# Queries projected in one pass over four banks, and two more steps by sums fed by moved weight preparations

## The chip, the cores and the metric

The kernel runs on one core of a Trainium2 chip. Its time is the device time of one execution in microseconds (us); the median of three runs counts. The engines are named as in the profile: PE (TensorE, matrix products), ACT (ScalarE), DVE (VectorE), POOL (GpSimd), SP (SyncE, which only issues loads here).

## What is computed

One layer of a streaming encoder on 256 tokens of width 2048, in float32: a gated linear attention in chunks of 64 tokens with 4 heads, then a squared-ReLU MLP, each behind an RMSNorm, and a final RMSNorm.

```python
def _gla_mixer(h, w_in, w_gate_up, b_gate, o_norm, w_out):
    proj = h @ w_in                       # 2048 x 6160: q 1024, k 1024, v 2048, r 2048, g_low 16
    q, k, v, r, g_low = jnp.split(proj, ...)
    log_a = jax.nn.log_sigmoid(g_low @ w_gate_up + b_gate) / GATE_TEMP
    ...                                   # k decayed within its chunk, a state per head, o = q @ state
    o = o * lax.rsqrt(jnp.mean(o * o, axis=-1, keepdims=True) + EPS) * o_norm
    return (o * jax.nn.silu(r)) @ w_out   # 2048 x 2048

def _sq_relu_mlp(h, w_up, w_down):        # 2048 x 8192, 8192 x 2048
    a = jax.nn.relu(h @ w_up)
    return (a * a) @ w_down

h = x + _gla_mixer(_rmsnorm(x, gla_norm), ...)
h = h + _sq_relu_mlp(_rmsnorm(h, mlp_norm), ...)
return _rmsnorm(h, final_norm)
```

## The kernel before

Every float32 operand of a projection is split in two parts, `hi` (rounded to the type that PE takes at full rate) and `lo` (the rest), and a product is made of three: hi by hi, hi by lo, lo by hi. All weights are streamed once. For 128 or 256 rows of weights, a *step*, SP loads 512 KB into one of 6 buffers `raw`; ACT copies it into a buffer `hi` (`L123`); DVE subtracts to get `lo` (`L136` in most stages, `L170` where 512 columns of two row blocks are taken at once, `L365` for sums); PE uses the two. There are 5 buffers each of `hi` and `lo`, so ACT and DVE work a few steps ahead of PE. A matmul moves 256 columns and is one instruction; a normal step has 24 of them.

**Steps by sums.** In `group` (four value and gate groups `x_group`, four output groups `out_group`, and in another form the MLP's second half) some steps of 256 x 512 weights are multiplied as 2 x 2 blocks by Winograd's scheme: seven block products in place of eight. POOL issues an accumulating DMA that adds one weight block onto another (`L335`), DVE makes further sums in `raw` (`L233`, `L234` in `weight_sums`), and a second pair of buffers takes the split sums (`L365`). PE first does three block products (9 matmuls); the other four (12 matmuls) are `pending` and come one step later. On the other side the activations need sums too, made once for a pair of row blocks `kp`: `X_FORMED = (0, 1, 4)` for the input, `FORMED = (0, 1, 6, 7)` for the attention's output.

**Preparations.** For some steps of the output groups the weight sums are made early, in stages where DVE has time, and written to DRAM: `make_sums` gives two jobs, `high` (load, three sums on DVE: `L252`, `L233`, `L234`; copy to `hi`, `L255`; POOL writes it to DRAM, `L256`) and `low` (DVE's `L259`, then POOL's write `L260`). `MADE_OUT` lists them as (group, kp), `MADE_AT` the places of a stage where they are done. The buffers `raw`, `hi` and `lo` of a preparation come from the same pools as those of the weight steps, so a `hi` of it is free for the next use when its write to DRAM has landed.

**Stages**, with their time in the profile: the first half of the values with the gate's low rank (4.5 to 51 us), keys (51.6 to 95.6), queries (95.6 to 139.8; two halves of 512 columns, each in two PSUM banks), the values' second half as groups V0 and V1 (139.8 to 167.7 to 188.4; the attention's scores are done within V0), the output gate's first half as groups G0 and G1 with the attention in them (to 238), its second half R (to 283), four output groups (to 371), the MLP (to 1009 and the tail).

The order within a stage is written by hand: `side` holds small jobs (gate, decays, sums of squares) of which `pump` takes one after each row block, `jobs` holds the preparations, `V0`, `V1`, `G0`, `G1` and `ORDER` give the order of the `kp` in a group and which go by sums, `between` what is done behind a step. The order on each engine then follows the program's, shifted by a scheduler; a buffer of a pool is given to the next tile that the scheduler sees fit. `OFF` and `even` place an operand at an address whose remainder by 128 bytes is 64 or, on purpose, 0; `FIRST` lets a group's first products take such a tile (`xe`).

Of the kernel before, what the change touches and what calls it, by code (L numbers as in the profile page):

```python
# [32 lines left out]
P = 128  # L33
T = 256
# [3 lines left out]
KT = D // P  # L38
# [3 lines left out]
KEYW = HEADS * DK  # L42
# [5 lines left out]
G = 1024  # L48
GT = 512
# [11 lines left out]
OFF = 48  # L61
# [8 lines left out]
def tile_gla_mlp(ctx, tc, x, xt, cols, w_vg, w_in, w_gate, w_out, w_up, w_down, final_norm, out):  # L70
    nc = tc.nc
# [53 lines left out]
    def slots():  # L125
        return [wpool.tile([P, SLOT], F32R, tag=i, name=i) for i in ("hi", "lo")]
# [84 lines left out]
    def turned(row, w, c0, even=(0,), acc=None):  # L211

        acc = acc or acc_banks(GT // P // 2)
        for kp in range(KT // 2):
            wh, wl = pair_of(w, kp, c0, even)
            for i in range(2):
                kt = 2 * kp + i
                ah, al = row(kt)
                for j in range(GT // P):
                    s = slice(j * P, (j + 1) * P)  # L220
                    o = acc[j // 2][:, j % 2 * T : (j % 2 + 1) * T]
                    for n, (u, m) in enumerate(((wh, ah), (wh, al), (wl, ah))):

                        nc.tensor.matmul(  # L224
                            o, u[:, i, s], m, start=kt == 0 and n == 0 and j % 2 == 0,
                            stop=kt == KT - 1 and n == 2, skip_group_check=True,
                        )
                if kt < KT - 1:
                    pump()
        return acc  # L230
# [3 lines left out]
        return nc.vector.tensor_tensor(u[:, 1::2], u[:, 1::2], u[:, 2:3].to_broadcast([P, 2, T]), op=ALU.subtract)  # L234


    MADE_OUT = ((1, 1), (2, 1), (3, 1), (3, 6))
    MADE_DOWN = ()
    MADE_AT = ((2,), (4,), (6, 10))
    made = {}  # L240

    def make_sums(key, src):
# [140 lines left out]
    def rows(w, c0, n=G, r0=0):  # L383
        return lambda kt: w[r0 + kt * P : r0 + (kt + 1) * P, c0 : c0 + n]
# [56 lines left out]
    def from_bank(dst, bank):  # L441

        b = bank.rearrange("p (i t) -> p i t", i=2)
        nc.scalar.copy(dst[:, :, WRAP:T], b[:, :, : T - WRAP])
        nc.vector.tensor_copy(dst[:, :, :WRAP], b[:, :, T - WRAP :])
# [222 lines left out]
    def extend_q(c):  # L668
        nc.scalar.copy(qt[:, c, T : T + CHUNK], qt[:, c, CHUNK:P])
        nc.vector.tensor_tensor(  # L670
            qt[:, c, T + CHUNK :].rearrange("p (b s) -> p b s", b=2),
            qt[:, c, P:T].rearrange("p (b s) -> p b s", b=2),
            dq[:, c, :].unsqueeze(2).to_broadcast([P, 2, CHUNK]),
            op=ALU.mult,
        )

    make = make_all()
    for half in range(2):
        jobs.extend(next(make))
        acc = turned(stream_x, w_in, half * GT, even=())  # L680
        for b in range(2):
            c0 = 4 * half + 2 * b
            from_bank(qt[:, c0 : c0 + 2], acc[b])
        side.extend([lambda c=c: extend_q(c) for c in range(4 * half, 4 * half + 4)])


    at = big.tile([P, 2, HEADS, 3 * P + 64], F32R, tag="C", name="at")
# [43 lines left out]
    def x_group(n, c0, order, summed, between, put, rows_of={}):  # L731
# [29 lines left out]
            order, summed, between, row, at_of, combine, put_all, filled=False, rows_of=rows_of,  # L761
        )

    V0 = (5, 6, 2, 0, 7, 3, 4, 1), (0, 4)
    V1 = (2, 5, 0, 3, 4, 6, 1, 7), (0, 4, 1)
    G0 = (2, 5, 0, 3, 4, 6, 1, 7), (0, 4, 1)
    G1 = (2, 0, 5, 4, 3, 1, 6, 7), (0, 4, 1)
    FIRST = {2: ((0, 1), (0, 0), (1, 0), (1, 1)), 3: ((0, 0), (0, 1), (1, 0), (1, 1))}
    rest = [side.popleft() for _ in range(len(side))]
    at_of_v = lambda c: lambda bank, t: put_v(bank, 512, t, G + c)  # L770
    x_group(0, 3 * KEYW, *V0, {
        0: lambda: [f() for f in rest[0:2]], 2: lambda: [f() for f in rest[2:4]],
        1: lambda: two_scores(0), 4: lambda: two_scores(2),
    }, at_of_v(0), FIRST)
# [119 lines left out]
    def begin_out(g):  # L894

        for t in range(NT):
            out_banks[g, t] = bank = psum_bank(out_ids[2 * (g % 2) + t])
            nc.scalar.copy(bank, h[:, t, g * GT : (g + 1) * GT])
# [5 lines left out]
        turn(on, turned_o, gain_o, 0, forms_o),  # L904
        turn(on, turned_o, gain_o, 1, forms_o, [psum_bank(i, "aux") for i in r_banks[4:]]),
    )])
    side.extend([nothing] * 3 + [lambda i=i: load_h(i % 2, i // 2) for i in range(4)] + [lambda: begin_out(0)])
    r_banks = list(acc_free)
    out_ids = r_banks[4:] + r_banks[:4]
    acc = natural(once_x, rows(w_in, 5 * KEYW), G, HALF, order=even_at(3, 5))  # L910
# [562 lines left out]
```

## Time and profile before

| | |
|---|---|
| median of 3 runs | 1040.99 us (1039.88 to 1041.95) |
| the profiled execution's own time | 1040.84 us, of which the span of the program's instructions is 1039.1 us |
| busy | PE 99%, DVE 87%, ACT 73%, POOL 13% |
| granted PE clock | 0.998 |
| moved by DMA | 240 MB, mean 231 GB/s |

The span runs from the first to the last instruction; 1.7 us of the execution lie around it. Busy shares are of the span. In the timeline a row is a run of equal instructions: its start, how long it lasts, engine, line, what it writes and reads, how many, and in brackets the idle time ahead of it and what ended that. Matmuls overlap, so the distance of two starts is what a matmul costs, not its length.

### The profile page before, as it was taken

Reading aid. Unit: us, or ns where it says so; the run is one execution under the profiler, and the core shown is the slowest. Engines: PE = TensorE matmul, PEld = TensorE weight load, DVE = VectorE, ACT = ScalarE, POOL = GpSimd, SP = SyncE. Lnnn points to the kernel's source line nnn. Section 1 sums busy time; section 2 is a strip of 40 time slices with the busy share of each in tenths; the row PEclk is TensorE's granted clock in tenths of the full one; section 3 lists DMA queues with packets and bytes.
Section 4 is the critical chain, followed back from the end, with each engine's and each line's share of the span. In section 5 each row is a group of like instructions: output and inputs, shape, how many; then the busy total and the mean of one; then the engine's idle time right before and its main releaser. Section 6 shows DMA issues by size and latency. Waiting matters only on the chain.

```text
span 1039.1 us, 23376 instructions
## 1 busy us (share of the span) xinstructions
PE 1030.4 (99%) x9019; PEld 1029.5 (99%) x9019; DVE 903.5 (87%) x1254; ACT 754.1 (73%) x1130; POOL 134.4 (13%) x180
## 2 busy tenths in 40 slices
PE   9999999999999999999999999999999999999997
PEld 9999999999999999999999999999999999999997
DVE  7769768898698866989989999999999999999887
ACT  7775556677576654688779788778778778778685
POOL 0000110210100001111111111111211111111100
PEclk9999999999999999999999999999999999999999
DMA  9967866758977876678888887887887888887772
GB/s 340 334 192 217 263 187 170 210 163 300 308 245 251 250 249 193 189 216 229 228 239 227 231 238 225 236 242 221 245 232 221 244 225 229 243 231 219 231 246 84
DMA packets 128591, 240.04 MB, mean 231 GB/s; under 512 B 11440, under 2 KB 30000, under 8 KB 128352
## 3 DMA queue, kind: packets, MB, share of 16 engines
q1 hardware_dynamic: 107456, 215.32, 64.2%
q0 software_dynamic: 20304, 21.64, 12.2%
q10 hardware_dynamic: 720, 1.60, 0.4%
q8 instruction: 70, 1.15, 0.4%
q14 instruction: 41, 0.34, 0.1%
HBM read 232.22 MB, written 6.29 MB: 230 GB/s over the span
## 4 chain that ended last, share of the span: by engine, by line
PE 99%; issue 0%; ACT 0%; DVE 0%; POOLq 0%; POOL 0%; DVEq 0%
PE up L1021 34%; PE acc L1021 28%; PE acc L305 16%; PE acc L181 10%; PE acc L224 6%; PE aux L224 2%; PE aux L181 1%; PE aux L843 1%; PE aux L696 1%; PE aux L399 0%; ACT sqf L1360 0%; PE acc L595 0%; DVE hf L1432 0%; POOLq L1469 0%; POOL rf L521 0%
## 5 line engine op out<-in xcount | busy, mean ns | idle before, releaser
L123 ACT CAST hi<-raw 128x1024 fp32r<-128x1024 f32 (+4 forms) x654 | 518.2, 822 | 201.1 <-DVE raw L233 66.4
L136 DVE TENSOR_TENSOR lo<-raw,hi 128x768 fp32r<-128x768 f32 (+4 forms) x228 | 233.1, 1032 | 53.6 <-ACT hi L123 50.8
L1021 PE MATMUL acc<-hi,act 128*128 128x256 f32 x1696 | 247.7, 276 | 0.0
L1021 PE MATMUL up<-hh,hi 128*128 128x256 f32 x1024 | 238.7, 276 | 0.0
L1021 PE MATMUL up<-hl,hi 128*128 128x256 f32 x1024 | 238.7, 276 | 0.0
L1021 PEld LDWEIGHTS acc<-hi,act 128*128 128x128 f32 x1696 | 217.6, 188 | 0.0
L170 DVE TENSOR_TENSOR lo<-raw,hi 128x1024 fp32r<-128x1024 f32 x160 | 194.4, 1218 | 22.5 <-ACT hi L123 21.6
L1021 PEld LDWEIGHTS up<-hh,hi 128*128 128x128 f32 x1024 | 192.3, 188 | 0.0
L1021 PEld LDWEIGHTS up<-hl,hi 128*128 128x128 f32 x1024 | 192.3, 188 | 0.0
L1231 POOL DMA_DIRECT2D raw<-in_w_down x112 | 97.1, 867 | 518.4 <-DMA raw<-in_w_down 206.2
L1291 DVE TENSOR_TENSOR lo<-raw,hi 128x1024 fp32r<-128x1024 f32 x112 | 136.3, 1217 | 1.1 <-ACT hi L123 1.1
L1021 PE MATMUL up<-hh,lo 128*128 128x256 f32 x1024 | 137.0, 276 | 0.0
L1021 PE MATMUL acc<-lo,act 128*128 128x256 f32 x848 | 133.9, 276 | 0.0
L1021 PEld LDWEIGHTS up<-hh,lo 128*128 128x128 f32 x1024 | 125.7, 188 | 0.0
L1021 PEld LDWEIGHTS acc<-lo,act 128*128 128x128 f32 x848 | 113.4, 188 | 0.0
L234 DVE TENSOR_TENSOR raw<-raw 128x512 f32<-128x512 f32 x137 | 94.5, 689 | 3.4
L233 DVE TENSOR_TENSOR raw<-raw 128x256 f32<-128x256 f32 x137 | 57.8, 422 | 13.1 <-DMA raw<-in_w_out 10.1
L181 PE MATMUL acc<-hi,xA 128*128 128x256 f32 (+1 forms) x376 | 55.6, 280 | 0.0
L181 PEld LDWEIGHTS acc<-hi,xA 128*128 128x128 f32 x376 | 49.3, 188 | 0.3 <-ACT hi L123 0.2
L224 PE MATMUL acc<-xA,hi 128*128 128x256 f32 x288 | 49.2, 276 | 0.0
L224 PEld LDWEIGHTS acc<-xA,hi 128*128 128x128 f32 x288 | 43.3, 188 | 0.0
L1148 ACT COPY sums<-acc 128x512 f32<-128x512 f32 x46 | 26.8, 583 | 22.6 <-PE acc L1021 22.5
(226 smaller groups left out, 1442.2 us busy)
## 6 DMA issues: line engine op xcount, KB each, us to landing
raw<-in_w_up SPq DMA_DIRECT2D x128, 512.0 KB, 4.3
raw<-in_w_down SPq DMA_DIRECT2D x224, 256.0 KB, 4.3
raw<-in_w_in SPq DMA_DIRECT2D x69, 512.0 KB, 4.6
raw<-in_w_down POOLq DMA_DIRECT2D x112, 128.0 KB, 5.1
raw<-in_w_out SPq DMA_DIRECT2D x22, 512.0 KB, 7.1
raw<-in_w_down SPq DMA_DIRECT2D x16, 512.0 KB, 5.2
raw<-in_w_vg SPq DMA_DIRECT2D x14, 520.0 KB, 8.6
raw<-in_w_out SPq DMA_DIRECT2D x24, 256.0 KB, 5.9
```

Source lines behind the costliest of these rows:

```text
L123: last_hi[0] = nc.scalar.copy(to, raw)
L136: last_lo[0] = nc.vector.tensor_tensor(lo[:, s], raw[:, s], hi[:, s].bitcast(F32), op=ALU.subtract)
L170: last_lo[0] = nc.vector.tensor_tensor(to[1], dst, to[0].bitcast(F32), op=ALU.subtract)
L181: newest[0] = nc.tensor.matmul(o[:, m], x, w[:, m], start=first and c == 0, stop=last, skip_group_check=True).ins
L224: nc.tensor.matmul(o, u[:, i, s], m, start=kt == 0 and n == 0 and j % 2 == 0, stop=kt == KT - 1 and n == 2, skip_group_check=True,)
L233: nc.vector.tensor_tensor(u[:, 2], u[:, 0], u[:, 2], op=ALU.subtract)
L234: return nc.vector.tensor_tensor(u[:, 1::2], u[:, 1::2], u[:, 2:3].to_broadcast([P, 2, T]), op=ALU.subtract)
L305: newest[0] = nc.tensor.matmul(bank[:, o + d : o + d + T], x, w[:, d : d + T], start=(not filled or bank in sums_banks) and bank.name not ...
L1021: newest[0] = nc.tensor.matmul(o, x, w, start=first, stop=last, skip_group_check=True).ins
L1148: last_end[0] = nc.scalar.copy(to, src).ins
L1231: nc.gpsimd.dma_start(out=raw[:, :T], in_=src[:, 0, T:], accum_op=ALU.add)
L1291: last_lo[0] = nc.vector.tensor_tensor(to[1][:, :G], u, to[0][:, :G].bitcast(F32), op=ALU.subtract)
```

## The change

1. **Queries in one pass.** The two halves become one loop over 16 row blocks with 1024 columns and four PSUM banks. A step is still 512 KB and 24 matmuls, 384 in all, and DVE's and ACT's work for a step is the same. The weights' `lo` is made by `L136` rather than `L170`, `pump` takes two side jobs per step, and all four banks are copied out at the end, where before two were copied out half way. The eight `extend_q` (a copy on ACT, a product on DVE) all come after the stage, in V0.
2. **Three preparations in the query stage** where there were two, one in V0 (places 5 and 6 of its steps) where there was none, one in R where there were two: five in place of four. The new one is (2, 6).
3. **A third step by sums in V0** (`kp` 1, with another order), and **a fourth in output group 2** (`kp` 6), which takes the new preparation.
4. In R the loads of `h` are queued two row blocks earlier.

```diff
-    MADE_OUT = ((1, 1), (2, 1), (3, 1), (3, 6))
+    MADE_OUT = ((1, 1), (2, 1), (2, 6), (3, 1), (3, 6))
-    MADE_AT = ((2,), (4,), (6, 10))
+    MADE_AT = ((1, 6, 11), (5,), (10,))
...
     make = make_all()
-    for half in range(2):
-        jobs.extend(next(make))
-        acc = turned(stream_x, w_in, half * GT, even=())
-        for b in range(2):
-            c0 = 4 * half + 2 * b
-            from_bank(qt[:, c0 : c0 + 2], acc[b])
-        side.extend([lambda c=c: extend_q(c) for c in range(4 * half, 4 * half + 4)])
+    jobs.extend(next(make))
+    acc = acc_banks(4)
+    for kt in range(KT):
+        wh, wl = weights(rows(w_in, 0)(kt), G, room=[a[:, OFF : OFF + G] for a in slots()])
+        xh, xl = stream_x(kt)
+        for j in range(8):
+            o = acc[j // 2][:, j % 2 * T : (j % 2 + 1) * T]
+            for n, (u, m) in enumerate(((wh, xh), (wh, xl), (wl, xh))):
+                nc.tensor.matmul(o, u[:, j * P : (j + 1) * P], m, ...)
+        if kt < KT - 1:
+            pump(2)
+    for b in range(4):
+        from_bank(qt[:, 2 * b : 2 * b + 2], acc[b])
+    side.extend([lambda c=c: extend_q(c) for c in range(8)])
...
-    V0 = (5, 6, 2, 0, 7, 3, 4, 1), (0, 4)
+    V0 = (5, 6, 2, 0, 4, 3, 1, 7), (0, 4, 1)
...
+    now = next(make)
     rest = [side.popleft() for _ in range(len(side))]
-    x_group(0, 3 * KEYW, *V0, {
-        0: lambda: [f() for f in rest[0:2]], 2: lambda: [f() for f in rest[2:4]],
+    between = {
+        0: lambda: [f() for f in rest[0:4]], 2: lambda: [f() for f in rest[4:8]],
         1: lambda: two_scores(0), 4: lambda: two_scores(2),
-    }, at_of_v(0), FIRST)
+    }
+    x_group(0, 3 * KEYW, *V0, {i: lambda i=i: (between.get(i, nothing)(), now[i]()) for i in range(8)}, at_of_v(0), FIRST)
...
-    side.extend([nothing] * 3 + [lambda i=i: load_h(i % 2, i // 2) for i in range(4)] + [lambda: begin_out(0)])
+    side.extend([nothing] + [lambda i=i: load_h(i % 2, i // 2) for i in range(4)] + [nothing] * 2 + [lambda: begin_out(0)])
...
-        out_group(g, ORDER[1], FORMED if g == 3 else (0, 1, 7), {
+        out_group(g, ORDER[1], FORMED if g > 1 else (0, 1, 7), {
```

What the change does to POOL's queue in V0 and V1 is seen in its order; `L335` are the accumulating loads of the steps by sums, and the brackets name the semaphores that an instruction waits for (DMASW are those of POOL's own DMAs, DMAHW those of SP's). Before, the three first rows are V0's `kp` 0 and 4 and V1's `kp` 0:

```order
L335 DMA raw_1976<-in_w_in 128x256 [waits DMAHW5_49,DMAHW3_49,DMAHW7_49,DMAHW1_49,DVE_49]
L335 DMA raw_2114<-in_w_in 128x256 [waits DMAHW3_49,DMAHW4_49,DMAHW2_49,DMAHW6_49,DMAHW0_49,DVE_49]
L335 DMA raw_2254<-in_w_in 128x256 [waits DMAHW0_49,DMASW4_49,DVE_49]
L335 DMA raw_2322<-in_w_in 128x256 [waits DMAHW5_49,DMAHW3_49,DVE_49]
L335 DMA raw_2388<-in_w_in 128x256 [waits DMAHW2_49,DMAHW6_49,DMASW0_49,DVE_49]
```

With the change the three first accumulating loads are V0's `kp` 0, 4 and 1, the fourth V1's `kp` 0; the write of V0's preparation (`made_1281`) stands behind that one:

```order
L335 DMA raw_1988<-in_w_in 128x256 [waits DMAHW3_49,DMAHW4_49,DMAHW2_49,DMAHW6_49,DMAHW0_49,DVE_49]
L335 DMA raw_2009<-in_w_in 128x256 [waits DMAHW3_49,DMAHW5_49,DMAHW2_49,DMAHW7_49,DMAHW1_49,DVE_49]
L335 DMA raw_2141<-in_w_in 128x256 [waits DMAHW1_49,DMAHW6_49,DMASW0_49,DVE_49]
L335 DMA raw_2283<-in_w_in 128x256 [waits DMASW7_49,DMAHW3_49,DMASW1_49,DVE_49]
L256 DMA made_1281<-hi_2137 128x1024 [waits DMASW2_49,Activation_49]
L260 DMA made_1281<-lo_2138 128x1024 [waits DMASW3_49,DVE_49]
L335 DMA raw_2351<-in_w_in 128x256 [waits DMAHW6_49,DMAHW0_49,DMAHW7_49,DMASW4_49,DVE_49]
```

So the two writes take the places 5 and 6 of these seven, and their issue waits until the load for V1's `kp` 0 is there.

On ACT, the end of V0 before has no preparation; `hi_2163` are the sums of `kp` 4, `hi_2196` is V1's first step, `L710` the scores' copies out of PSUM (two of the eight rows are shown):

```order
L123 CAST hi_2118<-raw_2114 128x768 [waits DMAHW4_49,DMAHW3_49,PE_49]
L123 CAST hi_2135<-raw_2133 128x1024 [waits DMAHW5_49,PE_49]
L123 CAST hi_2163<-raw_2114 128x2x256 [waits DMASW5_49,DVE_49,PE_49]
L123 CAST hi_2163<-raw_2114 128x2x256 [waits DVE_49]
L123 CAST hi_2196<-raw_2194 128x1024 [waits DMAHW6_49,PE_49,Activation_49]
L710 ACTIVATE at_1833<-aux_2046,r1_116 128x192 [waits PE_49]
L710 ACTIVATE at_1833<-aux_2047,r1_116 64x64 [waits PE_49]
```

With the change `hi_2137` is the preparation, `hi_2145` and `hi_2192` are the two parts of `kp` 1, `hi_2164` is `kp` 7, `hi_2225` V1's first step, `L720` the scores' copies:

```order
L255 CAST hi_2137<-raw_2132 128x1024 [waits DMAHW5_49,DVE_49,PE_49]
L123 CAST hi_2145<-raw_2141 128x768 [waits DMAHW7_49,DMAHW6_49,PE_49]
L123 CAST hi_2164<-raw_2162 128x1024 [waits DMAHW0_49,PE_49,Activation_49]
L720 ACTIVATE at_1837<-aux_2047,r1_116 128x192 [waits PE_49]
L720 ACTIVATE at_1837<-aux_2048,r1_116 64x64 [waits PE_49]
L720 ACTIVATE at_1837<-aux_2045,r1_116 128x192 [waits PE_49]
L720 ACTIVATE at_1837<-aux_2046,r1_116 64x64 [waits PE_49]
L123 CAST hi_2192<-raw_2141 128x2x256 [waits DMASW0_49,DMASW2_49,DVE_49,Activation_49]
L720 ACTIVATE at_1837<-aux_2048,r1_116 128x64 [waits DVE_49]
L720 ACTIVATE at_1837<-aux_2046,r1_116 128x64 [waits DVE_49]
L123 CAST hi_2192<-raw_2141 128x2x256 [waits DVE_49]
L123 CAST hi_2225<-raw_2223 128x1024 [waits DMAHW1_49,PE_49]
```

`hi_2192` was given the buffer of the preparation's `hi_2137`: its wait for DMASW2 is a wait until the write of `hi_2137` to DRAM has landed.

More of the change, by code (lines that the diff above doesn't have):

```diff
@@ L677, in tile_gla_mlp @@
     make = make_all()
-    for half in range(2):
-        jobs.extend(next(make))
-        acc = turned(stream_x, w_in, half * GT, even=())
-        for b in range(2):
-            c0 = 4 * half + 2 * b
-            from_bank(qt[:, c0 : c0 + 2], acc[b])
-        side.extend([lambda c=c: extend_q(c) for c in range(4 * half, 4 * half + 4)])
+    jobs.extend(next(make))
[6 more added lines that the diff above has]
+            for n, (u, m) in enumerate(((wh, xh), (wh, xl), (wl, xh))):
+                nc.tensor.matmul(
+                    o, u[:, j * P : (j + 1) * P], m, start=kt == 0 and n == 0 and j % 2 == 0,
+                    stop=kt == KT - 1 and n == 2, skip_group_check=True,
+                )
+        if kt < KT - 1:
[3 more added lines that the diff above has]
+    side.extend([lambda c=c: extend_q(c) for c in range(8)])
     at = big.tile([P, 2, HEADS, 3 * P + 64], F32R, tag="C", name="at")
```

## Prediction

> **What bounds the kernel now.** I read the page first, then the list of waits for PE alone, the table by stage, and the timelines of PE and DVE in V0 and V1. The page:
>
> ```profile
> PE 1030.4 (99%) x9019; PEld 1029.5 (99%) x9019; DVE 903.5 (87%) x1254; ACT 754.1 (73%) x1130; POOL 134.4 (13%) x180
> PE 99%; issue 0%; ACT 0%; DVE 0%; POOLq 0%; POOL 0%; DVEq 0%
> ```
>
> The last line is the chain that ended last: it is PE from end to end. PE's waits are a single row, at the start:
>
> ```profile
> PE aux L399 <- DVE ones L396: 1.1, 1, 1.1
> ```
>
> So every other engine is hidden, and what the change takes from them is worth nothing; what counts is the number of matmuls, the time of one, and any wait that appears. By stage (us, busy time and instructions of PE, its weight loads, DVE, ACT, POOL; then PE's clock, the DMA share, GB/s):
>
> ```profile
> 95.60:139.80 44.20, 44.20 (x392) 44.20 (x391) 33.37 (x51) 25.53 (x31) 5.72 (x21) 1.00 0.87 275
> 139.80:167.70 27.90, 27.90 (x237) 27.90 (x236) 18.53 (x37) 16.47 (x35) 2.57 (x3) 1.00 0.54 144
> 167.70:188.40 20.70, 20.70 (x185) 20.70 (x184) 19.13 (x26) 13.30 (x19) 1.74 (x2) 1.00 0.68 192
> 238.00:283.00 45.00, 45.00 (x399) 45.00 (x398) 33.16 (x45) 26.19 (x35) 5.70 (x8) 1.00 0.88 311
> 384.00:1009.00 625.00, 625.00 (x5515) 625.00 (x5513) 574.27 (x746) 483.62 (x708) 97.06 (x112) 1.00 0.80 228
> ```
>
> The rows are queries, V0, V1, R and the MLP. The MLP gives 625.00 / 5515 = 0.1133 us for a matmul. V1's DVE, 19.13 of 20.70, is the one engine near its limit here. In PE's timeline over V0:
>
> ```profile
> 145.25 3.25 PE L696 MATMUL aux<-qt,kab 128*128 128x128 f32 x24
> 148.25 0.72 PE L305 MATMUL acc<-hi,xe_gt 128*128 128x256 f32 x4
> ...
> 150.45 0.63 PE L305 MATMUL acc<-hi,xA 128*128 128x256 f32 x4
> ...
> 151.16 0.63 PE L305 MATMUL acc<-hi,xA 128*128 128x256 f32 x4
> 151.63 0.40 PE L305 MATMUL acc<-hi,xf 128*128 128x256 f32 x2
> 151.87 0.40 PE L305 MATMUL acc<-lo,xA 128*128 128x256 f32 x2
> 152.10 0.28 PE L305 MATMUL acc<-lo,xf 128*128 128x256 f32 x1
> ...
> 155.05 0.87 PE L305 MATMUL acc<-hi,xf 128*128 128x256 f32 x6
> 155.75 0.40 PE L305 MATMUL acc<-hi,xA 128*128 128x256 f32 x2
> 155.99 0.51 PE L305 MATMUL acc<-lo,xf 128*128 128x256 f32 x3
> 156.34 0.28 PE L305 MATMUL acc<-lo,xA 128*128 128x256 f32 x1
> ...
> 168.15 0.40 PE L305 MATMUL acc<-lo,xe_gt 128*128 128x256 f32 x2
> 168.39 0.62 PE L305 MATMUL acc<-hi,xA 128*128 128x256 f32 x4
> ...
> 169.07 0.62 PE L305 MATMUL acc<-hi,xA 128*128 128x256 f32 x4
> ...
> 179.72 0.39 PE L305 MATMUL acc<-lo,xE 128*128 128x256 f32 x2
> ```
>
> Two things are seen. A step by sums is 4+2+2+1 = 9 and 6+2+3+1 = 12 matmuls, 21 for a normal step's 24. And there are two paces: six matmuls take 0.71 us (150.45 to 151.16) behind the scores, but 0.68 (168.39 to 169.07) behind an `xe` tile, which is the MLP's pace; the slow one costs 0.005 us more for a matmul. A break in the stream sets the slow pace, and only such a tile ends it.
>
> **The change, part by part.**
>
> *Two steps by sums.* Each saves 24 - 21 = 3 matmuls, 6 in all, 6 x 0.1133 = 0.68 us, on the path. The two accumulating loads, DVE's sums and the second splits are hidden while PE is fed.
>
> *Queries.* 16 steps of 24 matmuls where there were 32 half steps of 12: 384 both times, 0. The hidden work is the same but for one preparation, priced as a rival. What is new on the path is the end: the scores of heads 0 and 1 come two V0 steps (48 x 0.1133 = 5.4 us) behind the last query matmul and now need all that is done for `qt`. The rows for it and for a preparation, and at the end POOL's issue of the accumulating loads (`L335`, ns: minimum, median, maximum) and the times from issue to landing of the 256 KB loads of steps by sums (`L334`) in V0, of POOL's writes of `hi` (`L256`) and of `lo` (`L260`):
>
> ```profile
> 139.33 0.56 ACT L444 COPY qt<-acc 128x480 f32<-128x480 f32 x1 [1.32 <-PE acc L224]
> 139.89 1.06 ACT L123 CAST hi<-raw 128x1024 fp32r<-128x1024 f32 x1
> 140.85 0.24 ACT L669 COPY qt<-qt 128x64 f32<-128x64 f32 x1
> 115.12 0.42 DVE L252 TENSOR_TENSOR raw<-raw 128x256 f32<-128x256 f32 x1
> 157.33 1.22 DVE L136 TENSOR_TENSOR lo<-raw,hi 128x1024 fp32r<-128x1024 f32 x1
> 166.06 0.69 DVE L234 TENSOR_TENSOR raw<-raw 128x512 f32<-128x512 f32 x1
> 174.78 1.22 DVE L136 TENSOR_TENSOR lo<-raw,hi 128x1024 fp32r<-128x1024 f32 x1
> L335 POOL DMA_DIRECT2D raw<-in_w_in x6: 853/860/876, 149.0 to 189.9; - x6
> DMA to landing us min/median/max: 2.8/3.7/5.2
> DMA to landing us min/median/max: 3.1/3.8/7.0
> DMA to landing us min/median/max: 6.5/6.9/7.1
> ```
>
> ACT has 4 x 0.56 + 8 x 0.24 + one split of 0.84 (three quarters of 1.06, and a little) = 5.0 us; two of the four banks are finished before the last query matmul, so about 3 us of it lie behind that, and the scores' 5.4 us cover them. Value 0; without that cover 1 us at most.
>
> *V0's preparation* is the part that can cost. Count from E, PE's last query matmul. PE: two steps to 5.4, scores to 8.4 (3.0 us, 145.25 to 148.25), then 24+9+9+12 = 54 matmuls at the slow pace (0.118) to 14.8, scores to 17.8, 24+12+9+24 = 69 more to 25.9. There it needs `hi_2192`, the second part of `kp` 1, and 8 matmuls later, at 26.9, its `lo`. The front part shows that `hi_2192` sits in the preparation's buffer, behind its write. DVE gets to the preparation when the sums of `kp` 4 are split: PE frees their buffer at 11.3, two ACT copies of some 0.6 and DVE's 1.22 end at 13.8; three sums (0.42, as much again for the second of that size, 0.69) to 15.4; ACT's copy (1.06) to 16.5. POOL issues the write behind the accumulating load of V1's `kp` 0, whose weights SP can fetch only when `kp` 4's `raw` is free at 13.8; the second of the two, queued 0.4 us later, lands 2.8 to 5.2 us after its issue, and POOL's issue of the accumulating load takes 0.86: the write starts at 17.9 to 20.4. With 3.1 to 4.3 us (three of the four rows behind 3.1/3.8/7.0) it lands at 21.0 to 24.7, with 7.0 at up to 27.4. Then two halves on ACT with two small score copies between them (some 1.8 us, an estimate from the 1.06 of a whole copy) and DVE's 1.22: `lo` is there at 24.0 to 27.7, or 30.4 in the worst row, against 26.9. So from 2.9 us early to 0.8 late, at worst 3.5 late. I take 0.2: the middle (25.9) is in time, but barely.
>
> The Trainium skill ("DMA: Bandwidth & Descriptors", Anatomy of one DMA) gives a DMA that GpSimd issues about 2.0 us and its bytes at 436 GB/s, mostly the receipt of the write. That would be 3.2 us for these 512 KB, an estimate, and by it the wait would be 0 and the time 1040.2. The trace agrees for the fastest `hi` write (3.1) and not for the `lo` ones (6.5 to 7.1).
>
> *Behind it* V1 starts without the head start that it had: `lo` of its first step was made at 157.33 to 158.55 and first used at 168.15, 9.6 us ahead; that of its fourth ended at 176.00 and was used at 179.72, 3.7 ahead. With the change DVE enters V1 at most 3 us ahead, with 1.6 us of it idle in the stage. I take that it keeps up (its work is unchanged, and a wait early in the stage gives time to the rest), and a wait of up to 1 us for the range.
>
> *R and output group 2.* R loses a preparation and gains slack, hidden: 0. The `h` loads are queued earlier on SP, behind forms that PE has used up by then: 0, or below 0.5 us of a raw load's cover. Group 2 loads 1 MB ready-made sums in place of 128 KB: group 3 does that already and PE doesn't wait in it: 0, at most 0.5.
>
> *Sum* against the profiled execution, 1040.84 (0.15 under the median of 1040.99): -0.68 + 0.2 = -0.5, 1040.4.
>
> **Rivals.**
>
> *V0's preparation is late and DVE falls behind in V1* (slower). For it: the buffer's wait and V1's 19.13 of 20.70 us; against: three of four writes are quick, and V0 moves only 144 GB/s. It decides once the write lands later than 23.8 behind E. Price: 1 to 3.5 us of waits, and each break sets the slow pace, at most the 183 matmuls of V1 (0.9 us), less the 0.68: 1041.5 to 1044.6, say 1042.8.
>
> *The query stage runs dry* (slower): a third preparation gives DVE 2.8 us more (33.4 to 36.2 of 44.2) and DMA 1.6 MB, 275 to 311 GB/s. R ran at 311 with no wait of PE, which speaks against it. A wait of 1.5 us and the slow pace for up to 400 matmuls (2.0): 1043.7. The Trainium skill, the same page under Bandwidth, puts what one core gets from HBM at about 358 GB/s; by that no wait, and R's 311 agrees.
>
> *The slow pace goes* (faster): behind each of the two scores some 60 matmuls run at it, 2 x 60 x 0.005 = 0.6 us, 1039.6; below 1038.9 only if further breaks elsewhere went as well. Nothing in the change aims at these; V0 keeps both scores and its `xe` tiles at the same steps.
>
> *Nothing is saved* since both steps' matmuls vanish behind something: only if PE waits there already, and it does not: 1040.84.
>
> **How the numbers follow.** Forecast 0.58, late preparation 0.23, dry queries 0.07, slow pace gone 0.09, nothing saved 0.03. Within 0.2% of 1040.99, about what a measurement of this kernel can tell from no change (its three runs span 0.2%), is 1038.9 to 1043.1. Slower than that: nearly half of the late preparation (0.11) and dry queries (0.07), 0.18. Faster: a part of the slow pace gone and the low end of the runs' scatter, 0.07. The rest, 0.75, is the same. The likeliest case alone gives 1039.8 to 1041.4; the range takes in the slow pace gone with that scatter, and most of the late preparation: 1038.9 to 1043.4.
>
> **What would show it.** Right: 9013 matmuls; PE's list of waits still without `L305` rows; `hi_2192` on ACT ending before PE's last V0 products; the queries' stage as long as before. Wrong: a wait of PE in V0 or V1 on ACT or DVE, ended by the landing of `made`; six matmuls in 0.71 us all through V1; a wait in the queries.

## The result and the profile after

The changed kernel takes 1044.3 us (median of 6 runs, 1043.23 to 1047.2) against 1040.92 (6 runs): ratio 1.0036, 95% interval 1.0025 to 1.0047. It is slower, by about 3.4 us, and above the forecast range. The profiled execution took 1045.51 with a span of 1043.7, the one before 1040.84 with 1039.1: 4.6 us to explain in the traces, since this execution lies 1.2 us over its median.

The page of the changed kernel, the lines that were shown of before:

```profile
PE 1032.9 (99%) x9013; PEld 1031.8 (99%) x9013; DVE 906.8 (87%) x1261; ACT 754.7 (72%) x1133; POOL 133.8 (13%) x183
PE 82%; DMA 1%; issue 1%; DVE 1%; ACT 0%; POOL 0%; POOLq 0%; DVEq 0%; ACTq 0%
```

The six matmuls are saved (9013 for 9019). But the chain that ended last is no longer PE alone: it leaves PE for DMA, ACT and DVE. PE's list of waits, which had the start row alone, now reads:

```profile
PE acc L305 <- DVE at L721: 1.4, 1, 1.4
PE aux L399 <- DVE ones L396: 1.1, 1, 1.1
PE aux L706 <- DVE qt L445: 0.6, 1, 0.6
PE acc L305 <- DVE lo L365: 0.5, 1, 0.5
```

Three new waits, 2.5 us together. In PE's timeline (line numbers are some 12 higher from the queries on: `L696` is now `L706`, `L710` and `L711` are `L720` and `L721`):

```profile
145.09 1.70 PE L706 MATMUL aux<-qt,kab 128*128 128x128 f32 x12
147.37 1.81 PE L706 MATMUL aux<-qt,kab 128*128 128x128 f32 x12 [0.58 <-DVE qt L445]
148.93 0.72 PE L305 MATMUL acc<-hi,xe_gt 128*128 128x256 f32 x4
...
167.23 0.40 PE L305 MATMUL acc<-hi,xA 128*128 128x256 f32 x2
168.15 0.62 PE L305 MATMUL acc<-lo,xf 128*128 128x256 f32 x3 [0.52 <-DVE lo L365]
168.61 0.28 PE L305 MATMUL acc<-lo,xA 128*128 128x256 f32 x1
168.72 0.63 PE L305 MATMUL acc<-hi,xe_gt 128*128 128x256 f32 x4
...
171.90 0.71 PE L305 MATMUL acc<-hi,xA 128*128 128x256 f32 x4 [1.41 <-DVE at L721]
```

The first scores take 148.93 - 145.09 = 3.84 us for 3.0. At the end of V0 the second part of `kp` 1 is late, and in V1's first step PE stops for 1.4 us behind 12 of its 24 matmuls. What ACT did meanwhile (its timeline, then DVE's, then POOL's):

```profile
157.60 1.04 ACT L255 CAST hi<-raw 128x1024 fp32r<-128x1024 f32 x1 [2.86 <-PE aux L706]
158.55 1.78 ACT L123 CAST hi<-raw 128x768 fp32r<-128x768 f32 x2
160.35 1.12 ACT L720 ACTIVATE at<-aux,r 128x192 fp32r<-128x192 f32 x4
165.29 0.62 ACT L123 CAST hi<-raw 128x512 fp32r<-128x512 f32 x1 [3.82 <-DMA made<-hi]
165.81 0.51 ACT L720 ACTIVATE at<-aux,r 128x64 fp32r<-128x64 f32 x2
166.22 3.24 ACT L123 CAST hi<-raw 128x512 fp32r<-128x512 f32 x4
169.49 0.51 ACT L720 ACTIVATE at<-aux,r 64x64 fp32r<-64x64 f32 x2
```
```profile
166.87 1.23 DVE L365 TENSOR_TENSOR lo<-raw,hi 128x1024 fp32r<-128x1024 f32 x1 [0.22 <-ACT hi L123]
168.01 3.22 DVE L136 TENSOR_TENSOR lo<-raw,hi 128x1024 fp32r<-128x1024 f32 x3
171.26 0.49 DVE L721 SCALAR_TENSOR_TENSOR at<-aux,r,at 64x64 fp32r<-64x64 f32 x2
```
```profile
159.31 0.86 POOL L335 DMA_DIRECT2D raw<-in_w_in  x1 [14.55 <-DMA raw<-in_w_in]
159.91 0.82 POOL L256 DMA_DIRECT2D made<-hi  x1
161.81 0.56 POOL L260 DMA_DIRECT2D made<-lo  x1 [1.07 <-DVE lo L259]
```

ACT stood 3.8 us until the preparation's `hi` had landed in DRAM (issued at 159.91, 5.3 us), and in its queue behind that stood the last copies of the scores (`L720`, 169.49). DVE started its late split (`L365`) at 166.87, had three whole splits in its queue behind it, and came to its half of the scores (`L721`) at 171.26. PE waited for that one; most likely V1's second bank still held those scores.

The rest is pace. The stage from V1's end to R's first transposes, by the table by stage (us, busy time and matmuls of PE), after and then before:

```profile
193.00:252.00 59.00, 59.00 (x503) 59.00 (x503) 52.45 (x78) 38.09 (x59) 7.98 (x12) 1.00 0.72 224
```
```profile
189.20:246.20 57.00, 57.00 (x506) 57.00 (x505) 51.51 (x77) 37.88 (x59) 10.53 (x12) 1.00 0.71 216
```

No wait and the full clock in both, yet 503 matmuls take 2.0 us longer than 506 did: the breaks had set the slow pace, G0's `xe` tile did not end it, and it lasted for 681 matmuls, from 171.90 to the transposes at 252.19 (before at 246.29):

```profile
246.29 1.91 PE L843 MATMUL aux<-ident,on 128*128 128x128 f32 x16
```
```profile
252.19 1.91 PE L855 MATMUL aux<-ident,on 128*128 128x128 f32 x16
```

So 5.9 us are lost by R: 3.9 of them by the attention's first product (193.93 before, 197.78 after), 2.0 behind it. The output groups 0, 1 and 2 give back 0.36, 0.26 and 0.34, the last being the three matmuls of its fourth step by sums; why the first two do is not shown. The `L181` products behind the MLP's last big stretch start at 1009.57 and 1014.49, 4.9 apart, and the tail gives back 0.3: 4.6.

### The profile page after: what moved, and what is told of

Read it like the earlier page. It is cut to its first block, busy times and chain, and to the rows that moved or that the text cites. A ratio compares the mean times of both kernels' runs of the same rounds, so it can differ in the third digit from the quotient of the medians.

```text
span 1043.7 us, 23405 instructions
## 1 busy us (share of the span) xinstructions
PE 1032.9 (99%) x9013; PEld 1031.8 (99%) x9013; DVE 906.8 (87%) x1261; ACT 754.7 (72%) x1133; POOL 133.8 (13%) x183
## 4 chain that ended last, share of the span: by engine, by line
PE 82%; DMA 1%; issue 1%; DVE 1%; ACT 0%; POOL 0%; POOLq 0%; DVEq 0%; ACTq 0%
PE up L1033 33%; PE acc L1033 28%; PE acc L305 14%; PE acc L181 6%; PE aux L181 1%; PE aux L855 1%; DMA made<-hi 1%; DMA raw<-in_w_in 0%; DVE lo L136 0%; ACT sqf L1372 0%; DVE lo L365 0%; ACT hi L123 0%; DVE hf L1444 0%; POOL raw L335 0%; POOLq L1481 0%
## 5 line engine op out<-in xcount | busy, mean ns | idle before, releaser
L123 ACT CAST hi<-raw 128x512 fp32r<-128x512 f32 (+4 forms) x656 | 517.3, 820 | 195.4 <-DVE raw L233 63.6
L136 DVE TENSOR_TENSOR lo<-raw,hi 128x768 fp32r<-128x768 f32 (+4 forms) x244 | 251.8, 1043 | 61.3 <-ACT hi L123 54.9
L170 DVE TENSOR_TENSOR lo<-raw,hi 128x1024 fp32r<-128x1024 f32 x144 | 175.1, 1219 | 17.1 <-ACT hi L123 16.8
L1303 DVE TENSOR_TENSOR lo<-raw,hi 128x1024 fp32r<-128x1024 f32 x112 | 136.4, 1218 | 1.1 <-ACT hi L123 1.1
L181 PE MATMUL acc<-hi,xA 128*128 128x256 f32 (+1 forms) x376 | 55.9, 281 | 0.0
L181 PEld LDWEIGHTS acc<-hi,xA 128*128 128x128 f32 x376 | 49.8, 189 | 0.0
L305 PE MATMUL acc<-hi,xA 128*128 128x256 f32 x248 | 40.2, 279 | 1.4 <-DVE at L721 1.4
L1146 DVE TENSOR_TENSOR act<-work,act 128x896 fp32r<-128x896 f32 (+2 forms) x32 | 34.7, 1083 | 5.2 <-ACT act L1145 5.1
```

The costliest lines, as they stand in the source:

```text
L123: last_hi[0] = nc.scalar.copy(to, raw)
L136: last_lo[0] = nc.vector.tensor_tensor(lo[:, s], raw[:, s], hi[:, s].bitcast(F32), op=ALU.subtract)
L170: last_lo[0] = nc.vector.tensor_tensor(to[1], dst, to[0].bitcast(F32), op=ALU.subtract)
L181: newest[0] = nc.tensor.matmul(o[:, m], x, w[:, m], start=first and c == 0, stop=last, skip_group_check=True).ins
L305: newest[0] = nc.tensor.matmul(bank[:, o + d : o + d + T], x, w[:, d : d + T], start=(not filled or bank in sums_banks) and bank.name not ...
L1146: on_vector(nc.vector.tensor_tensor(ol, x, oh.bitcast(F32), op=ALU.subtract))
```

## The experiments

Each run is the changed kernel with the edit shown, unless said; of longer edits the main lines are shown. Ratios are to the kernel before on the same chip.

**The parts apart.** The preparation of V0 back in R; V0 with two steps by sums and the preparation; the merge alone.

```diff
-    MADE_AT = ((1, 6, 11), (5,), (10,))
+    MADE_AT = ((1, 6, 11), (), (6, 10))
```

> The changed kernel, with the preparation of V0 done in R (places 6 and 10 there, as before); V0 keeps its third step by sums, the merged queries stay. Theory A (V0's preparation is the cause: the second part of kp 1 waits for its buffer's write, ACT and DVE then run late, and the broken stream keeps the slow pace of 118 ns until 252 us): PE's waits of 0.5 and 1.4 us behind V0 vanish, the 671 matmuls behind them are issued at 113.3 ns again (3.0 us), and the time is about 1040.5 (1040.0 to 1041.2); the wait of 0.6 us at the first scores stays. Theory B (three steps by sums in V0 are too much for DVE, with or without the preparation): waits of 1 us and more in V0 or V1 stay, and the time is 1043 or more.

Measured 1041.26, ratio 1.0001 (0.9993 to 1.0010), at the upper end of what theory A gave. No wait of PE is left from V0's end to R; 0.3 us at the first scores stay, and 0.4 us stand ahead of the output stage's transposes. Theory A holds so far: three steps by sums in V0 are not the trouble, the preparation is.

```diff
-    V0 = (5, 6, 2, 0, 4, 3, 1, 7), (0, 4, 1)
+    V0 = (5, 6, 2, 0, 7, 3, 4, 1), (0, 4)
```

> The changed kernel, with V0's order and its two steps by sums (kp 0 and 4) as before; the preparation stays in V0, 8982 matmuls. Here the second part of kp 4 sits in the preparation's buffer. Theory A (the preparation's buffer and write): waits of 1 to 2.5 us at the end of V0 or in V1 stay and the slow pace behind them as well: 1043 to 1045. Theory B (the third step by sums): the waits behind V0 vanish, about 1041.2.

Measured 1043.79, ratio 1.0031 (1.0019 to 1.0043): as slow with the preparation and without the third step. Its profiled execution, the fastest of its five at 1042.81, has no wait in V0 or V1 but a short one in G0:

```profile
PE aux L181 <- DVE on L807: 0.2, 1, 0.2
```

From there its pace is slow until R (376 matmuls in the 44.0 us from 205). The wait comes out later than expected, which the first runs do not explain.

The third is the kernel before with nothing but the merged queries (`MADE_AT` = ((1, 8), (), (6, 10)), four preparations):

> The kernel before with the queries merged over four banks and nothing else: its two early preparations lie at places 1 and 8 of the merged stage, V0, R and the output groups are as before, 8985 matmuls. Theory C (the merge costs only the wait at the second score block, since the scores take two of the queries' PSUM banks, whose copies stand on DVE behind a sum that waits for its load): one wait of about 0.6 us at 147 us, pace as before, 1041.7 (1041.3 to 1042.2). Theory D (the merge is where most of the loss is): 1043 or more, with the slow pace through V1. If the merge is free, 1040.9.

Measured 1040.81, ratio 0.9999 (0.9991 to 1.0008), PE's waits only the start row. The merge is free; theories C and D fall.

**The pace.** G0 begins with 12 matmuls on `xe` tiles in place of 6:

```diff
-    G0 = (2, 5, 0, 3, 4, 6, 1, 7), (0, 4, 1)
+    G0 = (2, 3, 0, 5, 4, 6, 1, 7), (0, 4, 1)
+    AGAIN = {2: ((0, 0), (1, 0), (1, 1), (0, 1)), 3: FIRST[3]}
```

> The changed kernel, with 12 matmuls in a row on the two xe tiles at the start of G0 (kp 2 and kp 3 side by side in its order, the xe tile of kp 2 last and of kp 3 first) in place of 6. All waits of PE stay. If the pace of 118 ns is a state that such tiles end, the 502 matmuls from 193 to 252 us fall to 113.3 ns: 2.2 us less, 1042.1 (1041.7 to 1042.6). If the pace comes from something else (the clock, loads of that stage, the order of the work), spacing stays 118 ns there and the time 1044.3.

Measured 1045.51 (1041.92 to 1048.85), ratio 1.0051 (1.0033 to 1.0069): not the 1042.1 that was expected. In its profiled execution (1041.92) the pace did what was expected, behind the wait of 1.1 us on `L721` in V1 slow, behind the 12 matmuls fast:

```profile
171.20:192.40 21.20, 21.20 (x183) 21.20 (x182) 19.73 (x29) 13.37 (x19) 2.59 (x3) 1.00 0.79 226
193.90:210.00 16.10, 16.10 (x144) 16.10 (x143) 13.46 (x22) 10.85 (x19) 4.25 (x7) 1.00 0.69 199
```

183 matmuls in 21.20 us are 0.1158 each, 144 in 16.10 are 0.1118 (a window counts a matmul more at its ends). The slow pace exists and can be ended there; what the new order of G0 cost in the slower executions has no trace.

The other trial put both `xe` tiles into `kp` 2, for 12 in a row behind the first scores, in V1 and in G0 (`EVEN = (4, 5)`, `FIRST = {2: ((0, 0), (0, 1), (1, 0), (1, 1))}`):

> The changed kernel, with the two xe tiles for row blocks 4 and 5 (both of kp 2) in place of 5 and 6, so that kp 2 begins with 12 matmuls on them in a row, behind the first scores, at the start of V1 and at the start of G0; the second scores have none behind them. The order of all steps stays. If 12 in a row always end the slow pace: 49 matmuls behind the first scores are faster by 4.6 ns (0.2 us), and from G0's start on the pace is 113.3 ns in every execution, 2.2 us less than in the profiled execution; the waits stay: about 1042.0 (1041.4 to 1042.8). If the pace is not a matter of these tiles, 1044.3.

Measured 1043.8, ratio 1.0027 (1.0018 to 1.0036): 0.5 less than the changed kernel, not 2.3. In the trace the pace was fast behind the first scores and again from 192.0, but PE still waited 0.9 us on `L721` and broke again at 210, after which it was slow to R. Ending the pace helps little while the breaks go on.

**The scores' wait.** The banks of the second head are exchanged with those of the sums:

```diff
-    x_banks = [list(acc_free)[i : i + 2] for i in (0, 4)]
-    x_sums = list(acc_free)[2:4]
+    x_banks = [list(acc_free)[i : i + 2] for i in (0, 2)]
+    x_sums = list(acc_free)[4:6]
```

> The changed kernel, with two pairs of PSUM banks exchanged: the second head of each score block goes to the queries' first two banks, which are copied out first, and the sums of V0 take the last two. Theory (the wait of 0.6 us in the first scores is the PSUM bank: the query stage now holds four, the scores need the last two of them, and DVE's copy of the last stands behind a sum that waits for its accumulating load): that wait is gone, the first 24 score matmuls take 3.0 us and not 3.84. The rest depends on the write of the preparation, which does not start earlier: PE comes 0.8 us sooner to the same waits, and the time stays at 1043.5 to 1044.3. Rival (the wait is for the data of qt): it stays. Rival (the late scores delay ACT and DVE in V0 and with them the preparation): the waits behind V0 shrink too, 1042 or less.

Measured 1044.73, ratio 1.0034 (1.0023 to 1.0045). The wait is gone and the time is not: PE's waits of 1.4 and 0.5 us behind V0 are there as before, to the tenth. The bank itself is likely but not shown: five of the fourteen profiled executions with merged queries and the old banks have a wait or gap there, none of the four with the new ones, and one execution without it proves little.

**The preparation, first the `hi` buffer.** V0's preparation gets a `hi` buffer outside the pool:

```diff
-            to.extend(slots())
+            to.extend(slots() if key != (None, 3, 1) else [mid.tile([P, G], F32R, tag="db", name="hi"), wpool.tile([P, SLOT], F32R, tag="lo", name="lo")])
```

> The changed kernel, in which only the hi buffer of V0's preparation is another one, of its own, so that kp 1's second part gets a buffer that is free; order and work of all engines are as in the changed kernel. Theory A1 (the wait for the buffer is the cause): ACT's wait of 3.8 us for the landing of the write is gone, PE's waits of 0.5 and 1.4 us with it, the xe tile at V1's start restores 113.3 ns, and the time is 1040.7 to 1041.7 (0.8 us of the wait at the scores stay). Theory A2 (the preparation's work of some 4 us on ACT and DVE makes the two late, whatever the buffer): waits of 1 us and more stay in V0 or V1, 1043 or more.

Measured 1045.04, ratio 1.0036 (1.0024 to 1.0048). ACT's wait and PE's waits in V0 and V1 are gone, and a larger one stands in G0. The waits of PE, and DVE's timeline in V1:

```profile
PE aux L181 <- DVE on L807: 1.9, 1, 1.9
```
```profile
166.59 0.49 DVE L721 SCALAR_TENSOR_TENSOR at<-aux,r,at 64x64 fp32r<-64x64 f32 x2
168.97 0.96 DVE L136 TENSOR_TENSOR lo<-raw,hi 128x768 fp32r<-128x768 f32 x1 [1.89 <-ACT hi L123]
```

(The scheduler used the free buffer to put ACT's copies for `kp` 1 and `kp` 7 ahead of the preparation's, so the order was not quite that of the changed kernel; it is the same in the run with both buffers outside the pools, below.) So A1 in this form falls, and A2 (too much work) seemed to stand. I then asked which part of the work. DVE's share of the preparation left out; and DVE's share alone, on data nobody needs:

```diff
-            nc.vector.tensor_tensor(u[:, 0], u[:, 0], u[:, 1], op=ALU.add)
+            if bare:
+                to.extend([mid.tile([P, G], F32R, tag="db", name="hi")] * 2)
+                nc.scalar.copy(to[0][:, :G], raw[0])
+                nc.gpsimd.dma_start(out=made[key][0], in_=to[0][:, :G].bitcast(F32))
+                return
```

> The changed kernel, with V0's preparation stripped of DVE's part: its load of 512 KB, ACT's copy (to a buffer of its own) and POOL's two writes stay, DVE's three sums and its subtraction (0.42 + 0.43 + 0.69 + 1.22 = 2.8 us) are left out, so one block of output group 3 is not computed as it should be. Theory E (2.8 us more on DVE where it has no slack: V0, V1, G0 and G1 come out late, and the debt reaches PE wherever it does first): back to the time with the preparation in R, 1041.3 (1040.7 to 1041.9), no wait of PE in V1 or G0. Theory F (the preparation's transfers, a raw buffer held and POOL's and SP's queues, are what delays V0 and V1): waits stay, 1043.5 or more.

```diff
+    def idle_sums():
+        for n in (T, T, GT):
+            nc.vector.tensor_tensor(idle[:, :n], some_v[:, :n], some_v[:, GT : GT + n], op=ALU.subtract)
+    now[5], now[6] = idle_sums, lambda: nc.vector.tensor_tensor(idle, some_v, some_v, op=ALU.subtract)
```

> The other half: the preparation is done in R, and in its place in V0 DVE alone makes four operations of the same sizes (256, 256, 512 and 1024 columns, 2.8 us) on data that lie in SBUF, whose results nobody uses; no load, no ACT copy, no write, no buffer of the pools. Theory E (DVE's time): as slow as the changed kernel, 1043 to 1045, with PE waiting in V1 or in G0 and the slow pace behind it. Theory F (transfers and buffers): 1041.3, as with the preparation in R.

Measured 1040.73, ratio 0.9999 (0.9990 to 1.0008), and 1040.72, ratio 1.0001 (0.9992 to 1.0010). Each half is free. E falls, and so does F as far as it means the transfers, the raw buffer and the queues of POOL and SP; the run without DVE's part took neither a `hi` nor a `lo` buffer of the pools. With DVE's idle work the table by stage for V0 and V1 reads

```profile
139.80:167.70 27.90, 27.90 (x237) 27.90 (x236) 23.34 (x50) 18.09 (x40) 2.81 (x4) 1.00 0.64 173
167.70:188.40 20.70, 20.70 (x185) 20.70 (x184) 19.77 (x27) 13.15 (x19) 2.58 (x3) 1.00 0.75 206
```

DVE is busy 19.77 of 20.70 us in V1, where it was 19.13 before, and PE does not wait there. Three more runs: all the work but without the chain from DVE's sums over ACT's copy to DVE's subtraction; the same with the raw buffer held; the chain whole, ACT's copy a place later.

```diff
+    def idle_sums():
+        load()
+        for n in (T, T, GT):
+            nc.vector.tensor_tensor(idle[:, :n], some_v[:, :n], some_v[:, GT : GT + n], op=ALU.subtract)
+    now[5], now[6] = idle_sums, lambda: (nc.vector.tensor_tensor(idle, some_v, some_v, op=ALU.subtract), store())
```

> The changed kernel's work in V0 in full, but without the preparation's chain: its load, ACT's copy (to a buffer of its own) and POOL's two writes are made as in the run without DVE's part, and DVE makes its four operations of the same sizes on other data, so that ACT's copy waits for no sum and DVE's last operation for no copy. One block of output group 3 is not computed as it should be. Theory G (the chain is what costs: DVE's sums, then ACT's copy, then DVE's subtraction, in queues that run in order, so that ACT's copies for the next steps wait behind the preparation's): 1040.8 (1040.3 to 1041.5), no wait of PE in V1 or G0. Theory H (each half fits, both together are too much work for V0 to G1): 1043.5 or more.

```diff
             else:
+                nc.vector.tensor_tensor(idle_of[0], raw[0], raw[0], op=ALU.subtract)
```

> As the run with the same work uncoupled, but DVE's last operation reads the preparation's raw buffer, so that one of the six raw buffers stays taken until then, as in the changed kernel (there the copy frees it). Theory G (the chain): 1040.8, as the run without this. Theory R (the raw buffer held through the scores delays SP's loads and the accumulating loads behind them): 1043 or more, with ACT or POOL waiting for loads of V1.

```diff
+        def copy():
             to.extend([mid.tile([P, G], F32R, tag="db", name="hi"), ...])
...
+        return high, copy, low
```

> The changed kernel with the preparation whole (its hi in a buffer of its own), in three jobs in place of two: load and sums at place 5, ACT's copy and the first write at place 6, the subtraction and the second write at place 7, so that ACT's copies for kp 1, kp 7 and the second part of kp 1 stand ahead of the preparation's. Theory G (ACT blocked behind the sums): ACT's wait of 2.9 us before the copy and PE's waits in V0, V1 and G0 go: 1041 to 1042. Theory H (too much work) or R (a raw buffer held, here still longer): 1043.5 or more.

Measured 1040.84, ratio 1.0003 (0.9993 to 1.0012); 1040.31, ratio 0.9999 (0.9989 to 1.0009); and 1044.37, ratio 1.0036 (1.0023 to 1.0049). H and R fall. G seemed right for the first two and wrong in the third, whose waits name something else (the whole program between 160 and 200 us, then PE):

```profile
DVE lo L136 <- DMA made<-lo: 2.4, 1, 2.4
```
```profile
PE aux L181 <- DVE oss L809: 1.5, 1, 1.5
```

DVE waits for the landing of the *second* write: the preparation's `lo` also comes from a pool of five, and the runs without the chain had taken none. (In the run with the own `hi` buffer the 1.89 us are put down to ACT, whose copy had ended at 166.10. There the preparation's `lo`, issued at 161.23, landed 7.6 us later, at 168.83, and DVE went on at 168.97, so it too seems to have waited for that buffer.) Two runs tell chain and buffer apart: the preparation whole, with both results outside the pools, and the run without a chain and with the raw buffer held, now with a `lo` buffer held too:

```diff
-wpool.tile([P, SLOT], F32R, tag="lo", name="lo")
+comb_x.rearrange("p f s -> p (f s)").bitcast(F32R)
```

> The changed kernel with the preparation whole, chain and all, but both its results in buffers outside the pools: hi as in the run with its own buffer, lo in the tile that the group's combination takes later. Theory A3 (buffers of the pools held until a write to DRAM has landed: with hi freed, DVE's splits in V1 still waited 1.9 to 2.4 us for the lo buffer, and the debt came out in G0): about 1040.8 (1040.3 to 1041.5), no wait of PE behind V0, fast pace from V1's start. Theory G (the chain DVE to ACT to DVE): 1043.5 or more, as with hi alone freed.

```diff
-                to.extend([mid.tile([P, G], F32R, tag="db", name="hi")] * 2)
+                to.extend([mid.tile([P, G], F32R, tag="db", name="hi"), wpool.tile([P, SLOT], F32R, tag="lo", name="lo")])
```

> The run with a held raw buffer and no chain, in which the second write takes its data from a lo buffer of the pool (DVE's last operation goes there, and reads no copy of ACT). V1's first step gets that buffer, so DVE's split for it waits until the write has landed. One block of output group 3 is not computed as it should be. Theory A3 (a pool buffer held by a write): slower again, 1042 or more, with DVE waiting for the landing of the write in V1. Theory G (the chain): 1040.8, as without the lo buffer.

Measured 1040.58, ratio 1.0000 (0.9991 to 1.0009), and 1046.22, ratio 1.0056 (1.0042 to 1.0069). PE's waits with both buffers outside the pools:

```profile
PE aux L706 <- DVE qt L445: 0.6, 1, 0.6
PE aux L855 <- DVE h L944: 0.5, 1, 0.5
PE acc L181 <- ACT hi L123: 0.3, 1, 0.3
PE aux L181 <- DVE on L807: 0.2, 1, 0.2
```

and with the `lo` buffer held and no chain, from all engines' waits between 160 and 200 us and then PE's:

```profile
DVE lo L136 <- DMA made<-lo: 4.0, 1, 4.0
```
```profile
PE aux L181 <- DVE on L828: 2.2, 2, 1.4
```

A3 is shown from both sides: the whole preparation in V0 is free as soon as its two results lie outside the pools, and one pool buffer behind a write is enough for more than 5 us (1046.22 against 1040.31 without it), with no chain at all. The `hi` buffer held alone was not run; what it does is seen in the changed kernel's own trace, ACT's 3.8 us above.

**Candidates.** The preparation in R with exchanged banks and both `xe` tiles in `kp` 2; the same with 6 matmuls on one in V1 and G0; and the kernel with both buffers outside the pools and exchanged banks.

> A candidate: V0's preparation done in R, the score banks exchanged, and the xe tiles for row blocks 4 and 5, together. Against the kernel with the preparation in R (1041.3): 0.5 us of the wait at the scores gone, 0.2 us of slow pace behind the first scores gone, perhaps 0.1 lost where the second scores have no xe tile: 1040.6 (1040.1 to 1041.0), that is, at most 0.3 us under the kernel before. Rival (the stages are bound by something else, or the sixth saved matmul is lost at output group 0 again): no faster than before.

> A candidate: as the earlier candidate (preparation in R, score banks exchanged, xe tiles for row blocks 4 and 5, 12 matmuls on them behind the first scores), but V1 and G0 begin with the xe tile of row block 5 alone, 6 matmuls, as in the kernel before, where V1's 170 matmuls fell to 113.3 ns behind it. If that holds here: 0.75 us less than the earlier candidate's 1040.54, 1039.8 (1039.4 to 1040.3), 0.05 to 0.1% under the kernel before. If the slow pace behind the scores outlasts V1's start again, 1040.5.

> The changed kernel, repaired in the two places that the runs point to: the preparation in V0 has both its buffers outside the pools, and the score banks are exchanged. Against the run with the buffers alone (1040.58): the wait of 0.6 us at the first scores is gone in the executions that have it. 1040.1 (1039.5 to 1040.7), that is up to 0.5 us under the kernel before; the six saved matmuls (0.68 us) would then show. If no faster than before, single short waits (G0's attention, the slow pace behind the scores) still take what is saved.

Measured 1040.54, ratio 0.9995 (0.9986 to 1.0004); 1040.88, ratio 1.0005 (0.9996 to 1.0014); 1040.02, ratio 1.0000 (0.9991 to 1.0009). All beat the changed kernel, none the kernel before. Why six matmuls less don't show is only half settled. Of the repaired kernel's 11 runs six lie between 1039.15 and 1040.02 and five between 1041.1 and 1042.3, where the 15 of before have 13 between 1040.0 and 1040.9: the gain seems to be there in half of the executions, and single short waits may eat it in the others. Its profiled execution (1041.13) has one in the first stage, on the input's first blocks, a stage that the change leaves as it was; what the other executions above 1041 waited for, no trace shows. PE's timeline there:

```profile
7.38 1.24 PE L181 MATMUL acc<-hi,xA 128*128 128x256 f32 x8 [1.19 <-ACT hi L123]
```

## Why the prediction was wrong

- *Steps by sums*: right. 6 matmuls went, and in output group 2, which nothing disturbed, three of them shrank the distance to before by 0.34 us, as 3 x 0.1133 says.
- *Queries, value 0*: right for the stage (the merge alone: 1.0) and wrong for its end. The cover counted ACT's work and missed DVE's order: a sum of V0's `kp` 0 waited 3.3 us for its accumulating load, and behind it, and behind a further sum and a split, stood the last copy of the banks (`L445` at 147.13). 0.84 us in the profile, within the bound of 1 that was given for a missing cover, and not in every execution.

```profile
144.31 0.42 DVE L233 TENSOR_TENSOR raw<-raw 128x256 f32<-128x256 f32 x1 [3.26 <-DMA raw<-in_w_in]
...
147.13 0.18 DVE L445 COPY qt<-acc 128x32 f32<-128x32 f32 x1
```

- *V0's preparation, 0.2*: the walk of the `hi` write was right almost to the end: the write was to start 17.9 to 20.4 behind E and started at 159.91 - 139.6 = 20.3, landed at 25.6 in 24.7 to 27.4, and `lo` was there at 28.5, late by half a us at PE. The rule of the Trainium skill ("DMA: Bandwidth & Descriptors", Anatomy of one DMA), 3.2 us for such a write by an estimate, did not hold here: 5.3 us for `hi`. In the 13 profiled executions with this write in V0 it took 3.9 to 6.3 us, so that the 3.1 of the range's fast end never came. The mistake was to take the middle of a range whose slow end came, and to price only PE's wait for that one tile. Two things were left out. In the queues of ACT and DVE the scores' last copies stood behind the same wait (1.4 us more). And the preparation's `lo` sat in a pool as well, behind a second write; in the changed kernel's own trace no wait is put down to that one, but it came out as soon as `hi` was freed.
- *Behind it, "I take that it keeps up"*: the step that failed. The sum had 0.2 us for the preparation's wait and nothing for what follows it. In the changed kernel PE stopped for 1.4 us in V1's first step, and 681 matmuls behind that stop ran at the slow pace (3.1 us). In the runs where `hi` was freed and `lo` still held, DVE's wait of 2 to 4 us in its in-order queue was not made up in V1 either: PE waited 1.9, 1.5 and 2.2 us in G0's attention. It was not the work: DVE did 19.77 us in V1 without a wait of PE when its buffers were free, and with both buffers outside the pools the time was 1040.58, near the 1040.4 that was forecast.
- *The price of a break*: not in the sum, and in the rival sized at 183 matmuls at the most (0.9 us). It was 681, 3.1 us at 0.0046 each, since G0's `xe` tile failed to end the slow pace. "Only such a tile ends it" was too strong on the prediction's own rows: an `xe` tile ran at 148.25, behind the first scores, and six matmuls still took 0.71 us at 150.45.
- *The rivals*: the late preparation was the right mechanism, with a price of 1041.5 to 1044.6 that held 1044.3, in part by luck: its 0.9 us for the pace is a third of the measured 3.1, and the wait at the scores was not in it. The queries did not run dry: PE has no wait there. The late preparation should have had the larger chance, and its point of decision (a write landing later than 23.8 behind E) was known to lie inside the forecast's own bounds.

## What to carry to other kernels

A tile that is written to DRAM holds its buffer until the write has landed, here 3.9 to 8.5 us in V0, and whoever is handed the buffer next waits inside an in-order queue; give such a tile a buffer of its own before asking whether an engine has time for the work. Follow all the tiles that a new step takes from a pool, not the one whose wait is visible: with one freed, the debt came out two stages later under another name. Where PE is the bound, price a break by the matmuls that run at the slower pace behind it, not by its own length.

## What the runs showed of the hardware

The slow pace (a matmul every 117.8 ns, against 113.3) is not always ended by an `xe` tile. Where V1 began with 6 matmuls on one and no wait fell near, it ended in 11 of 13 profiled executions, and 12 in a row failed in the one that tried it there; at G0's start 6 ended it in 4 of 5 and 12 in 3 of 3. Behind the first scores it is the other way: 6 were followed by the slow pace in 15 of 16 profiled executions, 12 by the fast one in 3 of 3. What decides is open. Behind R's first transposes stand 12 more matmuls on `xe` tiles, so the traces do not tell which of the two ends the slow pace there.

A wait of 1.9 us (G0, run with the own `hi` buffer) was followed by 3.7 us at a granted clock of 0.54, with matmuls 0.21 us apart; waits of 1.4 and 1.5 us elsewhere kept 1.00:

```profile
203.30:207.00 3.70, 3.70 (x19) 3.70 (x20) 3.26 (x6) 1.09 (x3) 2.11 (x2) 0.54 0.64 185
```

POOL's writes of 512 KB landed 5.3 us (`hi`) and 6.8 us (`lo`) after their issue in the changed kernel, and 8.0 us in the run with the `lo` buffer held, at a DMA share of 0.67 in V0 and 0.77 in V1 of the changed kernel. The share alone does not decide: in the changed kernel's query stage, at 0.86, two `hi` writes landed in 2.9 us and the `lo` writes in 6.9 to 7.7.
